# Moving DRAM sums, two gt2 steps, a pair of staging pages and one small write in a transformer block kernel

## The chip, the cores and the metric

The kernel runs on one core of one Trainium2 chip. A core has TensorE (matmuls; PE in the profile, with its weight loads as PEld), VectorE (DVE), ScalarE (ACT), GpSimd (POOL) and SyncE (SP), which here only issues DMAs. Sixteen DMA engines serve the core; DMAs are issued from the queues of SyncE, ScalarE and GpSimd, each in order. The metric is the time of one execution on the device in microseconds, from three runs and one profiled execution.

## The reference, cut to what matters

```python
mod = silu(c) @ w_ada + b_ada                      # 6 x 2048
sh1, sc1, gt1, sh2, sc2, gt2 = split(mod, 6)
h = rms_norm(x, g_mix) * (1 + sc1) + sh1
proj = h @ w_in                                    # xr, yr, q, k, v, f_logit
mix = concat(rms_norm(rglru(xr, yr)), rms_norm(forgetting_attention(q, k, v, f_logit)))
x = x + gt1 * (mix @ w_out)
h2 = rms_norm(x, g_ffn) * (1 + sc2) + sh2
gate, up = split(h2 @ w_up, 2)                     # w_up: 2048 x 11264
x = x + gt2 * ((silu(gate) * up) @ w_down)         # w_down: 5632 x 2048
```

There are 512 tokens and 2048 features, all in 32-bit floats. Each weight and each activation is split into a high and a low part (`hi` on ScalarE, `lo = raw - hi` on VectorE), and each product is three matmuls: hi by hi, hi by lo, lo by hi.

## The kernel before, in words

The work runs in one order: input projection, recurrence and attention by heads, output projection (four groups `wo0` to `wo3`), the upper product with `w_up`, the down product with `w_down`.

**The end of the output projection.** The modulation vectors come from dot products on VectorE: `ada_block` (L155) loads two pages of 512 KB of `w_ada` on SyncE's queue and multiplies them with silu(c). The last one of `SC2` gives `a2` (L902), with which `make_hr` (L905) makes the scaled input `hrh`, `hrl` of the upper product.

**The upper product.** The first 2 x 2 feature tiles are an ordinary product, two groups `up0` and `up1` (L1100), fed by `stream` (L257) through pages tagged `raw` (2 of them, 1 MB each). The other 40 feature tiles are done in 10 blocks of 4 (L1187). Each block is a 2 x 2 block product after Strassen and Winograd: seven products instead of eight, in the order 4, 5, 1, 7, 6, 2, 3. A product is eight steps j of six matmuls; two halves of four steps each. The weights of a block are four units, A, C, B and D, of two pages each (`load_unit`, L1130, SyncE's queue). `prod_weights` (L1151) loads A and C at product 4, B at product 1, D at product 2, and forms sums in place on VectorE: A += C for product 5, C += B for 7, A += B for 6, A += D for 3. Product 2 uses D itself. So C's pages come free in product 7, B's in 6, D's in 2 and A's in 3. Pages are of two kinds: `raw` (2) and `raw2` (4). `IN_RAW` says which units get `raw`: with (2, 4) modulo 8 it is B of an even block and A of an odd one.

`back` (L1175) brings the result of a block to the other layout in product 5 of the next block; `keep_act` (L1046) writes four forms of it to DRAM (`td`) on SyncE's queue.

**The DRAM sums.** The down product is also done by seven block products and needs two sums of quarters of `w_down` in DRAM (`s2d`, `s4d`), in 11 groups q. `sums24(q, n)` (L1078) issues at n = 0 four copies of 512 KB from SyncE's queue, ordered behind the last weight load that has been traced, and at n = 1, 2, 3 two adding DMAs each from GpSimd. Group 0 runs in `up0` and `up1` at `SUMS_STEPS`; the other ten in the blocks, one group every 13 halves from half 4 on (L1207).

**gt2.** The last modulation vector is made in the blocks. Its 64 pieces (4 rows r of c times 16 tiles i) are dealt out 6 or 7 to a block (`GT2_N`). Class `Gt2` (L178) loads at step (3, 3), that is product 7, step 3, up to six items from ScalarE's queue: a row of c whenever r changes, and pieces. Two items get a page with the tag `c`, the others one of four with the tag `d`, so later items must wait until a piece is used and its page comes free. `piece` runs one product on VectorE at the steps of `GT2_STEPS` ((4, 1) is product 6, step 1; 5 is product 2; 6 is product 3). Rows change in blocks 2, 5 and 7. `gt2_spread` (L1315) writes the 2048 sums to DRAM from 128 partitions (`k p -> p k`, 4-byte pieces, SyncE's queue) and reads them back spread over all partitions on GpSimd's queue.

**The down product.** `PHASES` (L1247) has four phases. In the first, products 4 and 5 alternate over 11 steps q; `dn_open` (L1262) loads per q a weight of 1 MB for each and two pages of activations from `td`. Product 4's weight goes to `raw`, product 5's to `raw2`; product 5 adds product 4's raw weight to its own (L1286), after which that `raw` page is free. One step is 24 matmuls.

**What sets the order.** The instructions of each engine and queue are put in order by a scheduler ahead of the run: by priority, among those whose inputs and pages it expects to be ready. `tc.high_priority(offset)` moves instructions up; `tc.issue_after(ins)` puts an instruction behind `ins` on its own engine and makes it wait for nothing else. On the chip each queue is in order: an instruction that waits for a page holds all behind it.

Of the kernel before, what the change touches and what calls it, by code (L numbers as in the profile page):

```python
# [54 lines left out]
STD = 2  # L55
X_STEPS = (13, 13, 13, 6)
KEEP = (2, 8, 2)
GT2_STEPS = ((4, 1), (4, 2), (4, 3), (4, 5), (4, 7), (5, 1), (5, 3))
GT2_N = (6, 6, 6, 6, 6, 6, 7, 7, 7, 7)
SUMS_AT, SUMS_PER = 4, 13  # L60
SUMS_STEPS = ((1, 8, 15), (6,))
BU_PART = (0, 5, 10, 16)
BUP_STEP = 3
NQ = FT // 4
# [7 lines left out]
def block_kernel(ctx, tc, xT, crow, adaT, vecs, bfr, w1, wyr, wqkv0, wqkv, wgate, wout, wup0, wups, wdn, outT):  # L72
# [411 lines left out]
    def add(hooks, n, *fns):  # L484
        hooks.setdefault(n, []).extend(fns)
        return hooks
# [613 lines left out]
    for gi in range(STD):  # L1100
        hk = {}
        if gi == 0:
            r1_sums, r1_spread = rstd_parts(ss1, D, "rstd_1", bank=acc)
            add(hk, BUP_STEP, up_bias_sum)
            add(hk, R1STEP[0], r1_sums)
            add(hk, R1STEP[1], lambda: r1.append(r1_spread()))
            add(hk, X_STEPS[3], lambda: x1_by_tokens(3))
        for i, n in enumerate(SUMS_STEPS[gi]):
            add(hk, n, lambda i=i + 3 * gi: sums24(0, i))
        for j in range(4):  # L1110
            add(hk, T_STEPS[gi][j], lambda j=j + 4 * gi: make_t(j))
        ps = fm_group(wup0[gi], list(range(KT)), hr, f"up{gi}", hooks=hk,
                      ps=[bank(gi + 1, f, f"up{gi}p{f}") for f in range(4)])
        up_last = lambda gi=gi, ps=ps: up_out(gi, ps)
        if gi < STD - 1:
            up_last()
# [4 lines left out]
    bp = ctx.enter_context(tc.tile_pool(name="bp", bufs=4))  # L1121

    U_A, U_C, U_B, U_D = range(4)
    IN_RAW = (2, 4)
    ORDER = (4, 5, 1, 7, 6, 2, 3)
    POST = 1900
    NBLK = (FT - 2 * STD) // 4
# [1 line left out]

    def load_unit(b, u):  # L1130
        tiles = []
        mine = len(loads) % 8 in IN_RAW
        loads.append((b, u))
        for hf in range(2):
            nm = f"uw{b}_{u}{hf}"
            if mine:
                t = wp.tile([P, 2048], F32, tag="raw", name=nm, bufs=RAW)
            else:
                t = bp.tile([P, 2048], F32, tag="raw2", name=nm)
            for i in range(2):  # L1140
                cs = slice(i * 1024, (i + 1) * 1024)
                ld = nc.sync.dma_start(out=t[:, cs], in_=wups[b, u, :, hf * 2048 + i * 1024:hf * 2048 + (i + 1) * 1024])
            up_loads.append(ld.ins)
            tiles.append(t)
        return tiles
# [39 lines left out]
    hk = {}  # L1185
    nprod = halves = 0
    for b in range(NBLK):  # L1187
# [6 lines left out]
        for i, p in enumerate(ORDER):  # L1194
# [3 lines left out]
            for j, hi, lo in prod_weights(p, b, un):  # L1198
                th, tl = T[p][j]
                for t in range(2):  # L1200
                    c_ = slice(t * P, (t + 1) * P)
                    mm(ps[t], th[:, c_], hi, j == 0, False)
                    mm(ps[t], th[:, c_], lo, False, False)
                    mm(ps[t], tl[:, c_], hi, False, j == 7)
                for fn in hk.get((i, j), ()):
                    fn()
                if j % 4 == 3:  # L1207
                    n = halves - SUMS_AT
                    halves += 1
                    if 0 <= n < SUMS_PER * (NQ - 1) and n % SUMS_PER % 3 == 0 and n % SUMS_PER < 12:  # L1210
                        sums24(1 + n // SUMS_PER, n % SUMS_PER // 3)
            if b + i == 0:
                up_last()
            if p in (4, 5, 1, 7):
# [34 lines left out]
    def dn_load(tag, blk, q, nm):  # L1249
        pool = wp if tag == "raw" else bp  # L1250
        raw = pool.tile([P, 2048], F32, tag=tag, name=nm, bufs=RAW if tag == "raw" else 4)
        src = {-2: s2d, -4: s4d}[blk][q] if blk < 0 else wdn[blk, q]
        for i in range(2):
            ld = nc.sync.dma_start(out=raw[:, i * 1024:(i + 1) * 1024], in_=src[:, i * 1024:(i + 1) * 1024])
        dn_loads.append(ld.ins)
        return raw

# [4 lines left out]
    def dn_open(ph, q):  # L1262
        prods = PHASES[ph]
        with tc.high_priority(offset=AHEAD):
            raws, ts = [], []
            for n, (p, blk, ix) in enumerate(prods):
                nm = f"dq{p}_{q}"
                raws.append(dn_load("raw2" if n or (len(prods) == 1 and q % 2) else "raw", blk, q, nm + "r"))
                tl, th = page(nm + "tl", "h"), page(nm + "th", "h")
                nc.sync.dma_start(out=tl, in_=td[ph][q][:, ix])  # L1270
                ts.append((th, tl))
        opened[ph, q] = raws, ts

# [40 lines left out]

    def gt2_spread():  # L1315
        gd = drp.tile([KT, P], F32, name="gt2d")
        nc.sync.dma_start(out=gd.rearrange("k p -> p k"), in_=mods[GT2])
        gv = gd.rearrange("(a k) p -> a k p", k=4)
        for a in range(4):
            g = page(f"gt2b{a}", "c")  # L1320
            nc.gpsimd.dma_start(out=g.rearrange("p (k m) -> p k m", k=4), in_=gv[a:a + 1].broadcast_to([P, 4, P]))
            gt2b.append(g)
# [25 lines left out]
    for ph, prods in enumerate(PHASES):  # L1348
# [8 lines left out]
        for q, n in steps:  # L1357
# [12 lines left out]
                    for f in TAIL_AT[q, k]:  # L1370
                        up_tail[f]()
            if n == 0:
                if (ph, q) == (0, 2):
                    gt2_spread()
        if ph == 0:
            q4, q5 = copies(ps[4], "q4_"), copies(ps[5], "q5_")
# [92 lines left out]
```

## Time and profile before

| | us |
|---|---|
| three runs | 2070.52, 2060.04, 2062.78 (median 2062.78) |
| profiled execution | 2061.59 |
| its span, first to last instruction | 2059.7 |
| TensorE busy | 2017.1 |
| VectorE busy | 1674.8 |
| ScalarE busy | 987.2 |
| GpSimd busy | 107.0 |

The mean granted TensorE clock was 0.992. The profile takes the span from the first instruction on; its page shows busy time by engine, the span in slices, the DMA queues, the chain of work that ended last and the costliest groups. Waits are listed as "engine, operation, line <- what ended the wait: total, times, longest". Windows show, for a stretch of time, each engine's busy time with its number of instructions, the granted clock (1.00 is full speed), the share of the DMA engines' time that was busy, and GB/s. A queue is written SPq or ACTq. `L255` is the matmul line, `L250` and `L251` are the two splits.

### The profile page before, as it was taken

What the parts mean: (1) busy time and instruction counts of PE and PEld (TensorE: products, weight loads), DVE (VectorE), ACT (ScalarE), POOL (GpSimd) and SP (SyncE); (2) the same over time, 40 slices, a digit from 0 to 9 for tenths busy, and PEclk for the clock granted to TensorE, in tenths of its full rate; (3) what the DMA queues carried; (4) which work ended last, traced back from release to release, by engine and by line L of the source; (5) the groups of instructions that cost most, each with busy time, mean ns of one, the idle gap of its engine ahead of it and who ended that gap; (6) DMA issues with size and microseconds to landing.
All of it is one profiled execution on the core that took longest, in us unless ns stands there. A gap on an engine that the chain in (4) does not pass through costs nothing.

```text
span 2059.7 us, 25583 instructions
## 1 busy us (share of the span) xinstructions
PE 2017.1 (98%) x9329; PEld 1695.0 (82%) x9329; DVE 1674.8 (81%) x2300; ACT 987.2 (48%) x1361; POOL 107.0 (5%) x138
## 2 busy tenths in 40 slices
PE   9999999999999989999999999999999899999999
PEld 7889998888888868888888877888778788888887
DVE  8999778986687659898798797887978877777796
ACT  4433447764522247544544444544445445545443
POOL 0000001111000000000000000000100100000000
PEclk9999999999999999999999999999999999999999
DMA  9989766667588884877977877596965577777793
GB/s 352 357 298 333 240 219 224 227 217 245 189 279 310 308 259 154 212 179 237 252 188 236 226 221 238 166 280 214 233 226 177 164 259 239 260 248 264 254 329 124
DMA packets 175714, 496.32 MB, mean 241 GB/s; under 512 B 20482, under 2 KB 43170, under 8 KB 171491
## 3 DMA queue, kind: packets, MB, share of 16 engines
q1 hardware_dynamic: 153316, 434.80, 61.6%
q0 software_dynamic: 11040, 39.59, 10.8%
q10 hardware_dynamic: 11232, 20.30, 2.8%
q8 instruction: 73, 1.20, 0.2%
q14 instruction: 53, 0.43, 0.1%
HBM read 458.93 MB, written 93.36 MB: 268 GB/s over the span
## 4 chain that ended last, share of the span: by engine, by line
PE 72%; DVE 9%; DMA 9%; issue 8%; ACT 1%; POOL 1%; SPq 0%; DVEq 0%; POOLq 0%; ACTq 0%
PE up_2p L255 5%; PE up_5p L255 5%; PE up_4p L255 5%; PE up_3p L255 5%; PE w1p L255 4%; PE up_1p L255 4%; PE up_7p L255 4%; DMA ada<-in_adaT 4%; PE up_6p L255 3%; PE dn6p L255 3%; PE dn3p L255 3%; PE dn1p L255 3%; PE dn2p L255 3%; PE dn7p L255 3%; PE dn5p L255 3%
## 5 line engine op out<-in xcount | busy, mean ns | idle before, releaser
L1149 DVE TENSOR_TENSOR uw<-uw,uw 128x2048 f32<-128x2048 f32 x80 | 182.6, 2282 | 0.0
L163 DVE SCALAR_TENSOR_TENSOR ada<-ada,c_b 128x1024 f32<-128x1024 f32 x96 | 116.2, 1220 | 43.3 <-DMA ada<-in_adaT 42.9
L250 ACT ACTIVATE up_0h<-uw 128x1024 fp32r<-128x1024 f32 x70 | 74.3, 1061 | 121.5 <-PE up_2p L255 23.6
L250 ACT ACTIVATE up_1h<-uw 128x1024 fp32r<-128x1024 f32 x70 | 74.4, 1063 | 108.4 <-PE up_6p L255 18.4
L251 DVE TENSOR_TENSOR up_0l<-uw,up_0h 128x1024 fp32r<-128x1024 f32 x70 | 85.4, 1220 | 35.3 <-ACT up_0h L250 35.3
L250 ACT ACTIVATE up_3h<-uw 128x1024 fp32r<-128x1024 f32 x70 | 74.4, 1063 | 79.7 <-PE up_2p L255 23.6
L251 DVE TENSOR_TENSOR up_1l<-uw,up_1h 128x1024 fp32r<-128x1024 f32 x70 | 85.3, 1219 | 30.3 <-ACT up_1h L250 30.3
L251 DVE TENSOR_TENSOR up_2l<-uw,up_2h 128x1024 fp32r<-128x1024 f32 x70 | 85.3, 1219 | 22.7 <-ACT up_2h L250 22.7
L250 ACT ACTIVATE up_2h<-uw 128x1024 fp32r<-128x1024 f32 x70 | 74.2, 1060 | 58.2 <-PE up_2p L255 16.6
L251 DVE TENSOR_TENSOR up_3l<-uw,up_3h 128x1024 fp32r<-128x1024 f32 x70 | 85.3, 1218 | 14.7 <-ACT up_3h L250 14.7
L1076 POOL DMA_DIRECT2D s2d<-in_wdn x44 | 36.6, 872 | 726.5 <-DMA s2d<-in_wdn 726.5
L201 DVE SCALAR_TENSOR_TENSOR gt<-gt,gt_None 128x512 f32<-128x512 f32 x64 | 43.1, 685 | 15.9 <-DMA gt<-in_adaT 15.9
L255 PE MATMUL w1p<-hpl,w1h 128*128 128x512 f32 x128 | 49.8, 389 | 0.0
L255 PE MATMUL w1p<-hph,w1l 128*128 128x512 f32 x128 | 49.8, 389 | 0.0
L255 PE MATMUL w1p<-hph,w1h 128*128 128x512 f32 x128 | 42.5, 392 | 0.0
L173 DVE SCALAR_TENSOR_TENSOR ada<-ada,c_b 128x1024 f32<-128x1024 f32 x32 | 39.0, 1218 | 4.1 <-ACT c_b L126 4.1
L173 DVE SCALAR_TENSOR_TENSOR adf<-adf,c_b 128x1024 f32<-128x1024 f32 x32 | 39.0, 1219 | 0.3 <-DMA adf<-in_adaT 0.2
L609 ACT ACTIVATE bt<-bt,nm 128x128 f32<-128x128 f32 (+3 forms) x32 | 18.0, 561 | 40.0 <-DVE nm L607 39.7
L688 DVE SCALAR_TENSOR_TENSOR ba<-bw,sh,ba 128x512 f32<-128x512 f32 x45 | 32.5, 746 | 3.8 <-DMA bw<-in_w 2.4
L954 DVE SCALAR_TENSOR_TENSOR bu_acc<-bu,mod,bu_acc 128x512 f32<-128x512 f32 x30 | 22.5, 748 | 13.5 <-DMA bu<-in_wup 13.0
L255 PEld LDWEIGHTS w1p<-hph,w1h 128*128 128x128 f32 x128 | 24.0, 188 | 5.4 <-ACT hph L416 0.3
L255 PEld LDWEIGHTS w1p<-hpl,w1h 128*128 128x128 f32 x128 | 24.0, 188 | 5.0
(2290 smaller groups left out, 6641.1 us busy)
## 6 DMA issues: line engine op xcount, KB each, us to landing
uw<-in_wups SPq DMA_DIRECT2D x160, 512.0 KB, 6.4
ada<-in_adaT SPq DMA_DIRECT2D x128, 512.0 KB, 5.7
s2d<-in_wdn POOLq DMA_DIRECT2D x44, 512.0 KB, 8.1
adf<-in_adaT SPq DMA_DIRECT2D x32, 512.0 KB, 6.4
gt<-in_adaT ACTq DMA_DIRECT2D x64, 256.0 KB, 6.2
s2d<-in_wdn SPq DMA_DIRECT2D x22, 512.0 KB, 10.5
s4d<-in_wdn SPq DMA_DIRECT2D x22, 512.0 KB, 9.9
s4d<-s2d POOLq DMA_DIRECT2D x22, 512.0 KB, 8.5
```

The costliest lines, as they stand in the source:

```text
L163: nc.vector.scalar_tensor_tensor(out=t, in0=t, scalar=1.0, in1=cs, op0=ALU.mult, op1=ALU.mult, accum_out=ac)
L173: nc.vector.scalar_tensor_tensor(out=t, in0=t, scalar=1.0, in1=c_b[:, cs], op0=ALU.mult, op1=ALU.mult, accum_out=ada_acc[j][:, hf, i:i + 1])
L201: nc.vector.scalar_tensor_tensor(out=t, in0=t, scalar=1.0, in1=c, op0=ALU.mult, op1=ALU.mult, accum_out=gt2_acc[:, r, i:i + 1])
L250: tail_hi.append(nc.scalar.activation(R(hi[:, :n]), raw_ap, AF.Copy).ins)
L251: tail_lo.append(nc.vector.tensor_sub(R(lo[:, :n]), raw_ap, hi[:, :n]).ins)
L255: nc.tensor.matmul(ps, lhsT=R(l), rhs=R(r), start=start, stop=stop)
L609: nc.scalar.activation(p[:, :n], p[:, :n], AF.Exp, scale=-1.0, bias=nm, accum_out=sm)
L688: nc.vector.scalar_tensor_tensor(out=ba[j], in0=src, scalar=s1, in1=ba[j], op0=ALU.mult, op1=ALU.add)
L954: nc.vector.scalar_tensor_tensor(out=a, in0=src, scalar=s2, in1=a, op0=ALU.mult, op1=ALU.add)
L1076: nc.gpsimd.dma_start(out=out[:, cs], in_=src[:, cs], accum_op=ALU.add)
L1149: nc.vector.tensor_add(d_, d_, s_)
```

## The change

It has four parts.

1. The DRAM sums of group 0 leave `up0` and `up1`; all 11 groups run in the blocks, one every 12 halves from half 2 on.
2. The sixth gt2 piece of a block moves from step (5, 1) to (5, 5), the seventh from (5, 3) to (6, 1).
3. Units C and D of every block get the `raw` pages, A and B the `raw2` pages; each weight load is ordered behind the load traced before it (A, C and B of block 0 only behind the first streamed load), and all loads of the down product behind the last one of the upper product.
4. `gt2_spread` is called at step (0, 4) of the down product, not (0, 2), and its write is ordered behind the last down weight load traced by then.

```diff
-GT2_STEPS = ((4, 1), (4, 2), (4, 3), (4, 5), (4, 7), (5, 1), (5, 3))
+GT2_STEPS = ((4, 1), (4, 2), (4, 3), (4, 5), (4, 7), (5, 5), (6, 1))
 GT2_N = (6, 6, 6, 6, 6, 6, 7, 7, 7, 7)
-SUMS_AT, SUMS_PER = 4, 13
-SUMS_STEPS = ((1, 8, 15), (6,))
+SUMS_AT, SUMS_PER = 2, 12
...
-        for i, n in enumerate(SUMS_STEPS[gi]):
-            add(hk, n, lambda i=i + 3 * gi: sums24(0, i))
...
-    IN_RAW = (2, 4)
+    IN_RAW = (1, 3)
...
-        mine = len(loads) % 8 in IN_RAW
+        mine = len(loads) % 4 in IN_RAW
...
-                ld = nc.sync.dma_start(out=t[:, cs], in_=wups[b, u, :, ...])
+                with tc.issue_after(up_loads[-1] if b or u == U_D else stream_loads[0]):
+                    ld = nc.sync.dma_start(out=t[:, cs], in_=wups[b, u, :, ...])
...
-                    if 0 <= n < SUMS_PER * (NQ - 1) and n % SUMS_PER % 3 == 0 and n % SUMS_PER < 12:
-                        sums24(1 + n // SUMS_PER, n % SUMS_PER // 3)
+                    if 0 <= n < SUMS_PER * NQ and n % SUMS_PER % 3 == 0 and n % SUMS_PER < 12:
+                        sums24(n // SUMS_PER, n % SUMS_PER // 3)
...
# dn_load, and the td load in dn_open
+            with tc.issue_after(up_loads[-1]):
...
# gt2_spread
-        nc.sync.dma_start(out=gd.rearrange("k p -> p k"), in_=mods[GT2])
+        with tc.issue_after(dn_loads[-1]):
+            nc.sync.dma_start(out=gd.rearrange("k p -> p k"), in_=mods[GT2])
...
-                if (ph, q) == (0, 2):
+                if (ph, q) == (0, 4):
                     gt2_spread()
```

More of the change, by code (lines that the diff above doesn't have):

```diff
@@ L1141, in load_unit @@
                 cs = slice(i * 1024, (i + 1) * 1024)
-                ld = nc.sync.dma_start(out=t[:, cs], in_=wups[b, u, :, hf * 2048 + i * 1024:hf * 2048 + (i + 1) * 1024])
+                with tc.issue_after(up_loads[-1] if b or u == U_D else stream_loads[0]):
+                    ld = nc.sync.dma_start(out=t[:, cs], in_=wups[b, u, :, hf * 2048 + i * 1024:hf * 2048 + (i + 1) * 1024])
             up_loads.append(ld.ins)
@@ L1253, in dn_load @@
         for i in range(2):
-            ld = nc.sync.dma_start(out=raw[:, i * 1024:(i + 1) * 1024], in_=src[:, i * 1024:(i + 1) * 1024])
+            with tc.issue_after(up_loads[-1]):
+                ld = nc.sync.dma_start(out=raw[:, i * 1024:(i + 1) * 1024], in_=src[:, i * 1024:(i + 1) * 1024])
         dn_loads.append(ld.ins)
@@ L1269, in dn_open @@
                 tl, th = page(nm + "tl", "h"), page(nm + "th", "h")
-                nc.sync.dma_start(out=tl, in_=td[ph][q][:, ix])
+                with tc.issue_after(up_loads[-1]):
+                    nc.sync.dma_start(out=tl, in_=td[ph][q][:, ix])
                 ts.append((th, tl))
```

## Prediction

> **What bounds the kernel now.** I read the page first, then TensorE's waits, then a table of windows cut at the start of each upper block product, then the chain of waits and SyncE's queue at the places where a window is too long.
>
> ```profile
> span 2059.7 us, 25583 instructions
> PE 2017.1 (98%) x9329; PEld 1695.0 (82%) x9329; DVE 1674.8 (81%) x2300; ACT 987.2 (48%) x1361; POOL 107.0 (5%) x138
> ```
>
> TensorE is the bound: 98% busy, 42.6 us of idle in the whole span. No part of the change adds or removes a matmul. So the change can only take away or bring waits of TensorE, and the slow matmuls that follow a wait.
>
> ```profile
> PE up0p L255 <- ACT hrh L908: 8.0, 1, 8.0
> PE dn4p L255 <- ACT dq_0w0h L250: 4.0, 1, 4.0
> 730.00:736.00 6.00, 2.16 (x4) 1.45 (x5) 5.64 (x11) 2.94 (x5) 1.22 (x2) 0.51 1.02 181
> 733.84 14.41 PE up0p L255 x48
> 1673.82 5.44 PE dn4p L255 x24
> 983.24:1061.39 78.15, 78.15 (x353) 64.58 (x353) 67.47 (x76) 38.30 (x44) 4.95 (x6) 1.00 0.80 226
> 1139.50:1219.38 79.88, 78.96 (x354) 64.40 (x353) 67.42 (x75) 38.07 (x44) 9.07 (x11) 1.00 0.94 251
> 1219.38:1303.41 84.03, 79.81 (x353) 65.53 (x353) 67.82 (x76) 38.20 (x44) 4.95 (x6) 0.98 0.74 218
> 1303.41:1381.61 78.20, 78.20 (x353) 64.50 (x353) 68.07 (x77) 38.41 (x44) 4.92 (x6) 1.00 0.74 217
> 1381.61:1466.89 85.28, 81.23 (x353) 65.97 (x353) 68.38 (x78) 38.20 (x44) 4.94 (x6) 0.96 0.74 220
> 1466.89:1546.69 79.80, 78.73 (x354) 64.43 (x353) 68.06 (x77) 38.10 (x44) 4.92 (x6) 1.00 0.81 226
> 1546.69:1627.00 80.31, 78.88 (x352) 64.00 (x351) 65.99 (x76) 36.56 (x43) 0.00 (x0) 1.00 0.47 139
> 1627.00:1755.40 128.40, 124.13 (x545) 101.73 (x546) 98.23 (x92) 65.78 (x82) 7.46 (x12) 0.99 0.75 256
> ```
>
> In a window's row stand its length, the engines' busy times, the granted clock, the DMA share and GB/s. A dense block takes 78.15 us (block 2). Blocks 4, 5, 7 and 8 take 1.73, 5.88, 7.13 and 1.65 us more: 16.4 us. Blocks 6 (78.20) and 2 lose nothing. Dense matmuls come 5.44 us per 24. In the standard product before the blocks, TensorE waits 8.0 us, and its next 48 matmuls take 14.41 us in place of 10.88, at a granted clock of 0.51: 11.5 us lost. The last two rows hold block 9 and the first phase of the down projection: 208.71 us, where a block (78.15), 22 steps of 5.44 and 16 transposes (1.74 by the row of 8 quoted below) make 199.6; 9.1 us lost. These three places, 37 us, are what the change can touch.
>
> **Part 1: the first group of DRAM sums leaves the standard product.**
>
> ```profile
> 705.02 0.63 SPq L1083 DMA_DIRECT2D s2d<-in_wdn  x1
> 711.05 1.47 SPq L152 DMA_DIRECT2D ada<-in_adaT  x2
> 685.22 8.73 DMA ada<-in_adaT
> 703.51 5.38 DMA ada<-in_adaT
> 712.19 17.88 DMA ada<-in_adaT
> 733.07 0.73 ACT hrh L908
> ada<-in_adaT SPq DMA_DIRECT2D x128, 512.0 KB, 5.7
> 712.00:718.00 6.00, 6.00 (x28) 4.96 (x27) 1.39 (x3) 1.06 (x1) 1.76 (x2) 1.00 1.03 347
> 722.64 1.12 ACT L924 ACTIVATE x1w<-x1p 128x512 f32<-128x512 f32 x2
> ```
>
> The chain of waits into the 8.0 us runs: last ada load (17.88 us, where the one before took 5.38 and the median is 5.7), two VectorE products, the modulation sum, hrh on ScalarE, TensorE. The four copies of 512 KB went out from 705.02 on, ahead of that load, and the DMA engines are full (share 1.03). The load itself cannot go earlier than 711.05, since its page is freed by VectorE then. With the copies gone it lands after 5.4 to 8.7 us (8.73 is the dearest of the ada loads ahead of it in the chain), at 718 to 721. hrh followed the landing by 3.0 us (712.19 + 17.88 to 733.07), so it could start at 721 to 724. ScalarE is busy with x1w until 723.76. TensorE's last matmul before the gap ends at 733.84 - 8.0 = 725.8. So the wait goes, and with it the slow clock: 11.5 us saved. If 1 us of wait remained, 10.5; never under 8.0 unless another wait ends late. What is late next is hrh behind x1w on ScalarE, about 2 us ahead of TensorE's need, less 0.7 for hrh itself.
>
> [...]
>
> **Part 2: eleven groups in the blocks, and later gt2 steps.** A group's four copies go on SyncE's queue right behind the weight load that was last when the group came up, and GpSimd adds as data land. By halves of a product (4+13n before, 2+12n after), they stand behind C in blocks 1 to 4, D in 4 to 7, B in 0 and 8 now; behind C in 0, 1, 6, 7, D in 1, 2, 7, 8 and B in 3, 4, 5 after.
>
> ```profile
> 1265.49 10.55 DMA gt<-in_adaT
> 1276.13 0.69 DVE L201 SCALAR_TENSOR_TENSOR gt<-gt,gt_None 128x512 f32<-128x512 f32 x1 [4.97 <-DMA gt<-in_adaT]
> 1429.37 12.96 DMA gt<-in_adaT
> 1442.43 0.69 DVE L201 SCALAR_TENSOR_TENSOR gt<-gt,gt_None 128x512 f32<-128x512 f32 x1 [4.05 <-DMA gt<-in_adaT]
> ```
>
> A group behind D puts its copies just ahead of the gt2 loads that reuse pages: they take 10.55 and 12.96 us, VectorE stands 4.97 and 4.05 us, and the splits behind it starve TensorE. Which piece it is differs. Blocks 2, 5 and 7 cross from one row of c to the next and load one row more. In block 5 the fifth piece waits, at step (4,7), which the change leaves; in block 7 the sixth, at (5,1), which goes to (5,5): four steps of six matmuls, or 5.44 us, later. That covers the 4.05. In the same way the sixth and seventh pieces of the other blocks are covered. On VectorE the pieces only trade places with the sums after product 6; the matmuls hide it, or else it costs up to 0.7 us per piece.
>
> After the change a D group meets a crossing in block 2 (fifth piece reused, as in block 5 now) and block 7. I price by the rows: block 2 as block 5 (5.88), block 7 and block 1 as block 4, which also has a C and a D group (1.73 each), blocks 3 and 5 (a B group behind a busy block) as block 8 (1.65 each), 4, 6 and 8 nothing. That makes 12.6 in place of 16.4: 3.8 saved. From both sides: if block 2 is also free and the rest cheap, 14 saved; if each D group costs 7.13, more lost than now (the third rival).
>
> **Part 3: pages of C and D, chained loads.** The pages of a unit are freed by the same splits as before, so each load waits for the same instruction. C of block 0 now takes the standard stream's pages, as B did; the last of it goes out where B's did (815.18, and earlier by what part 1 saves). Block 0 starts at 827 or later (983.24 less two blocks of at most 78.15), and C is wanted by its second product, 48 matmuls or 10.9 us on: nothing, hidden by product 4; without that cover it would be some 6 us once (5.7 for 512 KB). The loads' forced order (A, C, B, D) is the order in which pages come free: nothing. What it changes is the end: the pages for product 4's first two down weights are then D's, not A's.
>
> ```profile
> 815.18 0.81 SPq L1142 DMA_DIRECT2D uw<-in_wups  x2
> 1607.07 0.80 SPq L1254 DMA_DIRECT2D dq_2r<-in_wdn  x2
> 1614.19 0.38 SPq L1317 DMA_DIRECT2D gt2d<-mod  x1
> 1615.96 0.80 SPq L1254 DMA_DIRECT2D dq_0r<-in_wdn  x2
> 1622.00:1624.00 2.00, 2.00 (x10) 1.66 (x9) 0.41 (x1) 0.00 (x0) 0.00 (x0) 1.00 0.41 12
> gt2d<-mod SPq DMA_DIRECT2D x1, 8.0 KB, 12.3
> 1629.11 1.06 ACT dq_0w0h L250
> 1638.24 0.87 PE up_t L1178 x8
> 1645.70 0.81 SPq L1254 DMA_DIRECT2D dq_4r<-in_wdn  x2
> 1653.40 0.82 SPq L1254 DMA_DIRECT2D dq_3r<-in_wdn  x2
> 1687.16 0.81 SPq L1254 DMA_DIRECT2D dq_6r<-in_wdn  x2
> 1695.42 0.61 PE L255 MATMUL dn4p<-dq_6w0h,dq_6th 128*128 128x512 f32 x2
> ```
>
> Today product 4's first weight goes out at 1615.96, when A's page is freed, 1.8 us behind the gt2 write (8 KB in 4-byte pieces), which takes 12.3 us to land while the engines move 12 GB/s. ScalarE gets the weight at 1629.11, and TensorE waits the 4.0 us of the row above. D's page is freed at 1607.07 (product 5's third weight goes into it today). So after the change product 4's first weight goes out then, with no write ahead of it, and is there long before 1627: the start of the phase costs nothing.
>
> **Part 4: the gt2 write behind more loads.** It is now ordered behind the last load traced at step (0,4): product 5's fifth weight (1645.70 here). The next on SyncE is product 4's fourth weight, 7.7 us later (1653.40), for it waits for a page. The write would go out 0.8 us behind the former, so it blocks the queue for 12.3 - 6.9 = 5.4 us of that load's time, and the load lands 2.6 us after the block's end (as at 1615.96: 1614.19 + 12.3 = 1626.5, ScalarE begins 1629.11): 8.0 us after its issue. In the dense phase TensorE uses such a weight 8.26 us after the issue (1687.16 to 1695.42), and the splits take some 2.3 of that, an estimate from ScalarE's 1.06 with VectorE's step a little longer. So TensorE waits 2.0 us; or 5.0, if the weight of 1 MB issued just ahead holds the write up first (3.0 us at the 347 GB/s of the row in part 1). At the other end the block is hidden altogether. I take 3.5, and 2 us for block 9's VectorE and the clock: 5.5 of 9.1 lost remain, 3.6 saved (from -2 to 9).
>
> [...]
>
> **Sum.** 11.5 + 3.8 + 3.6 = 18.9 us off the profiled execution's 2061.6, or 2042.7; the median of the three runs (2062.8) is 1.2 above that execution: 2044.
>
> **The rivals.** 0.5% (10.3 us) is about what a measurement of this kernel can tell from no change.
>
> *The standard product keeps its wait.* hrh also needs ScalarE and VectorE, and the next two weights of 1 MB use the same queue; if the wait only shortens by 3 us, the sum is 18.9 - 8.5, or 2052.4. Against it: the load alone is out of line (17.88 against 5.7).
>
> *Almost all waits go.* The D groups drift past the gt2 loads and the write is hidden: 11.5 + 14 + 6 = 31.5 us, 2031. For it: block 6 has a D group and loses 0.05.
>
> *The D groups cost what the dearest does.* Four of them (blocks 1, 2, 7, 8) at 7.13 and the B groups of 3, 4 and 5 at 1.65 are 33.5 us where 16.4 are lost now: 17.1 more, against 15.1 gained elsewhere, 2065: slower. It turns slower where a D group costs over 6.6 us, and measurably at 9.2. Against it: blocks 4 and 6 have one and lose 1.73 and 0.05.
>
> *The write does not get behind what matters.* Ahead of it stand weights that are wanted late, behind it the one that is wanted next; if the block of 12.3 us comes through whole, the phase's start loses 12.3 where 9.1 was lost, 3.2 more: 2051.
>
> **How the numbers follow.** Forecast 0.60, wait kept 0.14, almost all gone 0.10, dear D groups 0.08, write in the way 0.08. The forecast's own range is 2036 to 2052 (parts 2 and 4 by their bounds, not both at once). 2033 to 2056 takes in half of the second rival and most of the first and last. Faster by over 0.5% (under 2052.5): 0.58 + 0.10 + 0.05 + 0.04 = 0.77. Same: 0.19. Slower by over 0.5%: half of the third rival, 0.04.
>
> **What would show it.** Right: no wait of up0p for hrh, its first 48 matmuls in 10.9 us, the last ada load in under 9 us; block 5 at 80 us or less and block 7 at 80; block 2 at 84; dn4p without a wait for dq_0; the gt2 write between product 5's fifth and product 4's fourth weight, and one wait of dn4p for dq_3 behind it. Wrong: up0p still waiting over 3 us; D groups costly in blocks 1 and 8; a new wait of over 6 us in the first phase.

## The result, and the profile after

The kernel after takes 2044.2 us, the median of four runs (2042.37 to 2046.33); the kernel before took 2061.9 beside it (2060.04 to 2070.52). The ratio is 0.9906, with a 95% interval of 0.9877 to 0.9936. The profiled execution of the kernel after took 2044.69 us. In its line numbers everything behind the changed constants stands one lower (the matmul line is L254).

The page, first its span and TensorE:

```profile
span 2043.0 us, 25569 instructions
PE 2012.8 (99%) x9329; PEld 1693.9 (83%) x9329; DVE 1676.8 (82%) x2300; ACT 987.4 (48%) x1361; POOL 104.7 (5%) x138
```

The span is 16.7 us shorter; TensorE is idle for 30.2 us of it in place of 42.6, and its busy time is 4.3 us shorter at an equal number of matmuls, with a mean granted clock of 0.995 in place of 0.992.

**The standard product.** SyncE's queue, its last load of `ada`:

```profile
714.04 1.47 SPq L151 DMA_DIRECT2D ada<-in_adaT  x2
```

The chain of waits (start, us, what):

```profile
728.82 10.88 PE up0p L254 x48
```

The load goes out 14.8 us ahead of `up0`; no wait stands there any more, and its first 48 matmuls take 10.88 us where they took 14.41.

**The blocks and the first down phase.** Windows cut at the first matmul of each block (1 to 5, 7 and 9 are shown), then the first and the second down phase. The columns are those of the prediction's windows, length first:

```profile
896.36:974.48 78.12, 78.12 (x353) 64.57 (x352) 67.67 (x75) 38.24 (x44) 8.23 (x10) 1.00 0.88 249
974.48:1053.34 78.86, 78.39 (x353) 64.49 (x352) 67.59 (x76) 38.41 (x44) 4.94 (x6) 1.00 0.75 219
1053.34:1139.02 85.68, 81.49 (x353) 65.33 (x352) 67.62 (x75) 37.92 (x44) 5.73 (x7) 0.98 0.85 231
1139.02:1217.13 78.11, 78.11 (x354) 64.57 (x352) 67.59 (x75) 38.41 (x44) 4.94 (x6) 1.00 0.82 221
1217.13:1296.15 79.02, 78.39 (x354) 64.50 (x352) 67.51 (x76) 38.39 (x44) 5.76 (x7) 1.00 0.85 239
1374.31:1452.71 78.40, 78.40 (x354) 64.44 (x352) 68.01 (x78) 38.40 (x44) 8.22 (x10) 1.00 0.91 252
1530.87:1609.00 78.13, 78.13 (x354) 64.57 (x352) 68.83 (x79) 39.25 (x46) 1.24 (x2) 1.00 0.63 204
1609.00:1738.48 129.48, 124.51 (x546) 102.26 (x544) 95.70 (x90) 63.10 (x79) 7.48 (x12) 0.97 0.75 232
1738.48:1858.18 119.70, 119.70 (x530) 99.07 (x528) 90.47 (x78) 59.27 (x72) 0.00 (x0) 1.00 0.73 248
```

A block without a wait takes 78.13 us. Blocks 5, 7 and 8, which lost 14.7 us before, now lose 1.2; block 2 loses 0.7; block 3, which lost nothing, loses 7.6. Blocks 0 to 8 lose 9.5 us in place of 16.6 (these windows begin a tenth of a microsecond elsewhere than the prediction's, which is why 16.4 became 16.6). Block 9 and the first down phase take 207.6 us, 8.0 over the 199.6 that the prediction worked out; before they lost 9.1.

**Where the down phase waits now.** TensorE's longest wait, then the chain into it:

```profile
PE dn4p L254 <- ACT dq_3w0h L249: 4.9, 1, 4.9
```

```profile
1629.76 12.13 DMA dq_3r<-in_wdn
```

gt2's write on SyncE's queue and the read on GpSimd's of what was written, in order of time:

```profile
1621.98 0.54 SPq L1318 DMA_DIRECT2D gt2d<-mod  x1
1639.86 2.21 POOL L1322 DMA_DIRECT2D gt2b<-gt2d  x4 [13.38 <-DMA gt2d<-mod]
```

Two windows, while the write is under way and after the wait:

```profile
1628.00:1632.00 4.00, 4.00 (x19) 3.30 (x19) 2.79 (x2) 2.02 (x2) 0.00 (x0) 1.00 1.30 54
1642.00:1648.00 6.00, 4.86 (x11) 3.36 (x12) 4.84 (x4) 2.63 (x3) 0.07 (x1) 0.50 1.03 413
```

`dn4p` no longer waits for its first weight (`dq_0`) but for its fourth (`dq_3`), issued 7.8 us behind gt2's write. The write goes out at 1621.98, and its reader is released at 1639.86, 17.9 us later. In the first window the DMA engines are busy (share 1.30) and move 54 GB/s. After the wait the clock is at 0.50 for some 6 us.

**Block 3.** SyncE's queue around the end of block 2 (the first copies of two groups), then GpSimd's last sums of the earlier group, of the later one and, for comparison, of the group after that:

```profile
1020.95 0.57 SPq L1082 DMA_DIRECT2D s2d<-in_wdn  x1
1049.75 0.50 SPq L1082 DMA_DIRECT2D s2d<-in_wdn  x1
1054.78 0.82 POOL L1075 DMA_DIRECT2D s4d<-s2d  x1 [3.00 <-DMA s2d<-in_wdn]
1088.43 0.81 POOL L1075 DMA_DIRECT2D s4d<-s2d  x1 [5.06 <-DMA s2d<-in_wdn]
1161.56 0.81 POOL L1075 DMA_DIRECT2D s4d<-s2d  x1 [2.43 <-DMA s2d<-in_wdn]
```

The two longest pieces of the chain into the wait:

```profile
1081.71 12.23 DMA td<-tu
1093.97 11.14 DMA gt<-in_adaT
```

A group behind D (from 1020.95) and a group behind the next block's B (from 1049.75) stand 29 us apart; the other neighbours begin 59 to 86 us apart. The earlier group's last sum goes out at 1054.78, when the later group's copies are already in flight. The later group's last sum goes out at 1088.43, 38.7 us behind its first copy; the next group, also behind a B but alone, needs 26.2 (1135.40 to 1161.56). So the later group's sums still run when block 3 writes `td`. A write of `td` then takes 12.23 us, the gt2 load that gets its page another 11.14, and the splits behind them on ScalarE and VectorE come late (ScalarE stands 3.13 and 4.73 us ahead of two of them).

**What differs without the change.** TensorE reached `up0` at 725.8 before and at 728.8 after, 3.0 us later, though up to there the DMA queues differ only by the six transfers of group 0 (705 to 717), which the change takes away. Among the traces of this study it came there between 724.7 and 731.4. Most of this lies in the attention stage, behind which TensorE came at 494.5 in place of 491.5; the window from 200 to 500 us, first in the kernel after:

```profile
200.00:500.00 300.00, 288.51 (x1563) 265.39 (x1562) 240.61 (x456) 177.81 (x327) 28.85 (x34) 0.98 0.69 230
```

And in the third experiment below, which came to `up0` at 724.7:

```profile
200.00:500.00 300.00, 290.47 (x1578) 266.61 (x1577) 242.17 (x459) 178.71 (x327) 31.54 (x35) 0.99 0.71 231
```

TensorE does 2.0 us more work there in the second. In the span, then, the 16.7 us are 11.5 (standard product) + 7.1 (blocks 0 to 8) + 1.1 (block 9 and first down phase) - 3.0 (run to run).

### The profile page after: what moved, and what is told of

It is laid out like the page before. It is cut to its first block, busy times and chain, and to the rows that moved or that the text cites. A ratio compares the mean times of both kernels' runs of the same rounds, so it can differ in the third digit from the quotient of the medians.

```text
span 2043.0 us, 25569 instructions
## 1 busy us (share of the span) xinstructions
PE 2012.8 (99%) x9329; PEld 1693.9 (83%) x9329; DVE 1676.8 (82%) x2300; ACT 987.4 (48%) x1361; POOL 104.7 (5%) x138
## 4 chain that ended last, share of the span: by engine, by line
PE 81%; issue 7%; DVE 6%; DMA 4%; POOL 1%; ACT 1%; SPq 0%; DVEq 0%; POOLq 0%; ACTq 0%
PE up_2p L254 5%; PE up_3p L254 5%; PE up_5p L254 5%; PE up_4p L254 5%; PE up_1p L254 5%; PE w1p L254 4%; PE up_7p L254 4%; PE up_6p L254 4%; PE dn6p L254 3%; PE dn3p L254 3%; PE dn1p L254 3%; PE dn2p L254 3%; PE dn7p L254 3%; PE dn4p L254 3%; PE dn5p L254 3%
## 5 line engine op out<-in xcount | busy, mean ns | idle before, releaser
L249 ACT ACTIVATE up_0h<-uw 128x1024 fp32r<-128x1024 f32 x70 | 74.3, 1062 | 115.6 <-PE up_7p L254 18.9
L250 DVE TENSOR_TENSOR up_0l<-uw,up_0h 128x1024 fp32r<-128x1024 f32 x70 | 85.5, 1222 | 30.2 <-ACT up_0h L249 29.9
L250 DVE TENSOR_TENSOR up_3l<-uw,up_3h 128x1024 fp32r<-128x1024 f32 x70 | 85.4, 1220 | 12.3 <-ACT up_3h L249 12.3
L254 PE MATMUL w1p<-hph,w1l 128*128 128x512 f32 x128 | 49.8, 389 | 0.0
L254 PE MATMUL w1p<-hpl,w1h 128*128 128x512 f32 x128 | 49.8, 389 | 0.0
L254 PE MATMUL w1p<-hph,w1h 128*128 128x512 f32 x128 | 42.5, 392 | 0.0
L953 DVE SCALAR_TENSOR_TENSOR bu_acc<-bu,mod,bu_acc 128x512 f32<-128x512 f32 x30 | 22.5, 749 | 12.9 <-DMA bu<-in_wup 12.5
L415 ACT ACTIVATE hph<-x,A 128x512 fp32r<-128x512 f32 x16 | 11.6, 723 | 36.0 <-DVE A L412 36.0
L620 ACT ACTIVATE pT<-pt 128x512 f32<-128x512 f32 (+3 forms) x32 | 13.2, 435 | 31.8 <-PE pt L616 31.8
```

The costliest lines, as they stand in the source:

```text
L249: tail_hi.append(nc.scalar.activation(R(hi[:, :n]), raw_ap, AF.Copy).ins)
L250: tail_lo.append(nc.vector.tensor_sub(R(lo[:, :n]), raw_ap, hi[:, :n]).ins)
L254: nc.tensor.matmul(ps, lhsT=R(l), rhs=R(r), start=start, stop=stop)
L620: nc.scalar.activation(pT[:, qs], pt[:, qs], AF.Copy)
L953: nc.vector.scalar_tensor_tensor(out=a, in0=src, scalar=s2, in1=a, op0=ALU.mult, op1=ALU.add)
```

## The experiments

Ten kernels were run. What each loses, from windows like those above, is in this table; "b9 + phase 1" is what block 9 and the first down phase take over 199.6 us, "std" the wait ahead of `up0` and the slow clock behind it. A dense block counts 78.13 us (block 0: 76.16), which leaves some 0.2 us open in a sum over nine blocks. Medians are of 4 to 10 runs, of one run where marked.

| kernel | median | std | blocks 0-8 | of it block 3, 4 | b9 + phase 1 | phase 2 |
|---|---|---|---|---|---|---|
| before | 2061.9 | 11.5 | 16.6 | 0.0, 1.7 | 9.1 | 0 |
| after | 2044.2 | 0 | 9.5 | 7.6, 0.0 | 8.0 | 0 |
| 1: before + sums | 2050.7 | 0 | 13.6 | 4.4, 0.0 | 8.4 | 0 |
| 2: after, write in rows | 2031.0 | 0 | 5.7 | 4.9, 0.0 | 0.0 | 0.3 |
| 3: after, old gt2 steps | 2041.6 | 0 | 9.6 | 7.4, 0.0 | 7.7 | 0 |
| 4: after, old pages | 2047.1 | 0 | 10.0 | 6.3, 0.0 | 9.9 | 0 |
| 5: before + write moved | 2060.5 (one) | 10.5 | 15.9 | 0.1, 0.0 | 9.1 | 0 |
| 6: after, write from ScalarE | 2040.2 (one) | 0 | 8.4 | 7.1, 0.0 | 7.6 | 0 |
| 7: after, a group every 13 halves | 2042.3 | 0 | 7.8 | 0.0, 6.5 | 6.8 | 0 |
| 8: rows, groups spread | 2028.4 | 0 | 1.4 | 0.0, 0.0 | 0.2 | 0.2 |
| 9: after, late write in pieces | 2040.7 | 0 | 8.6 | 7.3, 0.2 | 0.0 | 4.5 |
| 10: before + sums + pages | 2050.5 | 0 | 15.9 | 6.4, 2.2 | 7.8 | 0 |

**1. The sums alone.** The kernel before with part 1 and the new places of the groups; pages, order, gt2 steps and write as before.

```diff
-SUMS_AT, SUMS_PER = 4, 13
+SUMS_AT, SUMS_PER = 2, 12
-        for i, n in enumerate(SUMS_STEPS[gi]):
-            add(hk, n, lambda i=i + 3 * gi: sums24(0, i))
```

> The kernel before with part 1 of the change alone (all eleven groups of sums in the blocks, every 12 halves from half 2). Theory: TensorE's wait before the first standard product goes, and with it the slow clock behind it: 11.5 us saved there. The gt2 write still stands ahead of the first down weight: dn4p waits about 4 us for dq_0 and the first down phase takes 128 us. With the old pages the copies of a D group stand between the two halves of the next block's unit A, ahead of the gt2 loads: blocks 1 and 7 lose 2 to 7 us each, all blocks together 12 to 19, as before. Time 2050 (2046 to 2053). Rival: the sums' new place is all there is to the change, blocks and down phase included: 2044.

2050.66 us (2046.3 to 2054.5, ten runs), ratio 0.9954 (0.9939 to 0.9969). The chain of waits at the start of `up0`:

```profile
725.88 10.88 PE up0p L254 x48
```

The standard product loses nothing, which is the whole of part 1's 11.5 us, shown with this part alone. The blocks still lose 13.6 of 16.6 us, 5.1 of them in block 7, but only 0.7 in block 1, for which 2 to 7 had been expected. The profiled execution (2046.34) was among the fastest of the ten, so its blocks are rather on the cheap side.

**2. gt2's write in rows.** The kernel after, with the 128 x 16 sums transposed on TensorE and written as 16 rows of 512 bytes in place of 2048 pieces of 4. The scheduler put it later as well, into the second down phase.

```diff
+        pt = rgp("gt2t")
+        nc.tensor.transpose(out=pt[:KT, :P], in_=mods[GT2], identity=ident)
+        gt2row = cp.tile([P, P], F32, name="gt2row")
+        nc.vector.tensor_copy(out=gt2row[:KT, :], in_=pt[:KT, :P])
-            nc.sync.dma_start(out=gd.rearrange("k p -> p k"), in_=mods[GT2])
+            nc.sync.dma_start(out=gd, in_=gt2row[:KT, :])
```

> The changed kernel with the gt2 write made of 16 rows of 512 bytes (TensorE transposes the 128x16 sums first, VectorE copies them out) in place of 2048 pieces of 4 bytes, at the same place in the queue. Theory: the 4-byte pieces are what held up product 4's fourth weight; the wait of dn4p for dq_3 (4.9 us, and the slow clock behind it) goes, the first down phase takes 122 to 123.5 us in place of 129.5, and the time falls by 6 to 7: 2038. Rival: the fourth weight is late because its page comes free late; the wait stays, 2044.

2030.99 us (2030.45 to 2032.36), ratio 0.9855 (0.9831 to 0.9879): 13 us less than the kernel after, where 6 to 7 had been expected. The windows of block 3, of the first and of the second down phase:

```profile
1051.32:1134.33 83.01, 80.95 (x354) 65.50 (x352) 67.62 (x75) 38.17 (x44) 5.73 (x7) 0.98 0.87 235
1603.50:1724.99 121.49, 121.49 (x545) 100.76 (x544) 95.61 (x90) 62.99 (x79) 5.29 (x8) 1.00 0.71 240
1724.99:1844.95 119.96, 119.96 (x530) 98.95 (x529) 90.74 (x79) 59.39 (x72) 2.19 (x4) 1.00 0.75 255
```

The first down phase is dense: 121.49 us, all of it busy, 8.0 less. The rest of the 13 us lies where the write cannot reach: 3.8 in blocks 0 to 8 and 1.7 ahead of `up0` in these profiles. Up to there the DMA queues of the two kernels have the same order, so this is a difference between executions; but the four runs of each kernel lie closer together than that, and where it comes from is not shown. Form and place of the write were both changed; experiments 6 and 9 take them apart.

**3. The old gt2 steps.**

```diff
-GT2_STEPS = ((4, 1), (4, 2), (4, 3), (4, 5), (4, 7), (5, 5), (6, 1))
+GT2_STEPS = ((4, 1), (4, 2), (4, 3), (4, 5), (4, 7), (5, 1), (5, 3))
```

> The changed kernel with the old gt2 steps (sixth piece at (5,1), seventh at (5,3)). Theory: the later steps only matter where a reused page is refilled late, which now is block 7 alone (D group and a change of rows): 2 to 4 us more there, the other blocks as in the changed kernel; 2046.5. Rival A: the later steps are what freed the blocks: blocks 5 and 7 or those with a D group (1, 2, 7, 8) lose 4 to 7 each again, 2052 or more. Rival B: they do nothing: 2044.

2041.59 us (2040.72 to 2043.75), ratio 0.9907 (0.9882 to 0.9931). My theory fell: the blocks lose 9.6 us, as with the new steps (9.5), and block 7, whose sixth piece the later step was to cover, loses nothing:

```profile
1370.80:1448.93 78.13, 78.13 (x354) 64.57 (x352) 68.22 (x78) 38.23 (x44) 8.22 (x10) 1.00 0.92 256
```

VectorE waits 0.9 us for gt2 loads in this block, where it waited 5.2 in the kernel before, and TensorE does not feel it; so part 2's later steps cover nothing.

**4. The old pages.** The kernel after with B and A alternately in the `raw` pages, as before; the forced order of the loads is kept.

```diff
-    IN_RAW = (1, 3)
+    IN_RAW = (2, 4)
-        mine = len(loads) % 4 in IN_RAW
+        mine = len(loads) % 8 in IN_RAW
```

> The changed kernel with the old choice of pages (B of an even and A of an odd block in the raw pages), its chained load order kept. Theory: in blocks 1 and 7 the copies stand again between the halves of the next block's unit A, ahead of the gt2 loads, and the blocks lose 2 to 4 us more each; product 4's first weight goes out about 9 us later than in the changed kernel, when A's page comes free, but with no write ahead of it and lands in time (dn4p waits under 1 us for dq_0); 2048. Rival A: the pages bring nothing by themselves: 2044. Rival B: the late page alone costs the start of the down product 3 us or more, whatever the write does.

2047.12 us (2041.40 to 2049.86), ratio 0.9931 (0.9908 to 0.9954). Blocks 0 and 9:

```profile
822.94:900.43 77.49, 76.79 (x337) 62.91 (x336) 69.48 (x77) 36.53 (x41) 0.81 (x1) 1.00 0.50 161
1534.15:1614.61 80.46, 78.92 (x353) 64.34 (x352) 68.64 (x79) 39.19 (x46) 1.48 (x2) 1.00 0.61 193
```

Block 9 is 2.3 us longer than in the kernel after, and block 0, 76.16 without a wait, 1.3. The pages are worth 2 to 3 us (2.4 by the table, 2.9 by the medians, whose runs overlap), mostly at the two ends of the row of blocks. The theory's 2 to 4 us each in blocks 1 and 7 did not come: both lose nothing. That TensorE does not wait for `dq_0` was as expected.

**5. The write moved, alone.** The kernel before with part 4.

```diff
-        nc.sync.dma_start(out=gd.rearrange("k p -> p k"), in_=mods[GT2])
+        with tc.issue_after(dn_loads[-1]):
+            nc.sync.dma_start(out=gd.rearrange("k p -> p k"), in_=mods[GT2])
-                if (ph, q) == (0, 2):
+                if (ph, q) == (0, 4):
```

> The kernel before with part 4 alone: gt2's write of 2048 pieces goes behind product 5's fifth weight load instead of behind product 4's fourth. In the kernel before, the last block and the first down phase lost 5.6 and 3.6 us to it, 9.1 us together. The prediction's theory (behind more loads the write meets less): 5.5 us together, about 3.6 us less. Theory after the experiments on form, place and queue (the pieces delay whatever load is next behind them by about the same time): the loss of the block moves into the phase, block 9 loses 0 to 2.5 us, the phase 7 to 9 us, together 8 to 11 us, no gain over 1.5 us. The std product's wait of about 8 us and the losses of the other blocks stay as before.

One run of 2060.5 us beside 2061.0 for the kernel before. TensorE's two longest waits:

```profile
PE up0p L255 <- ACT hrh L908: 8.4, 1, 8.4
PE dn4p L255 <- ACT dq_3w0h L250: 4.8, 1, 4.8
```

Block 9 and the first down phase:

```profile
1545.33:1625.35 80.02, 78.92 (x354) 64.35 (x352) 68.72 (x79) 39.22 (x46) 0.00 (x0) 1.00 0.49 169
1625.35:1754.00 128.65, 123.86 (x545) 101.78 (x544) 95.63 (x90) 63.09 (x79) 7.48 (x12) 0.97 0.76 237
```

Block 9 loses 1.9 us in place of 5.6, the phase 7.2 in place of 3.6: 9.1 together, exactly what the kernel before loses. Part 4 by itself moves a loss and removes none.

**6. The write from ScalarE's queue.**

```diff
-        with tc.issue_after(dn_loads[-1]):
-            nc.sync.dma_start(out=gd.rearrange("k p -> p k"), in_=mods[GT2])
+        with tc.issue_after(tail_hi[-1]):
+            nc.scalar.dma_start(out=gd.rearrange("k p -> p k"), in_=mods[GT2])
```

> The kernel after, with gt2's write of 2048 pieces of 4 bytes issued from ScalarE's queue instead of SyncE's, at about the same time of the first down phase. In the kernel after, product 4's fourth weight came late behind this write and the first down phase lost 8.0 us. Theory of the queue (the loads wait because they stand behind the write on SyncE's own queue): the fourth weight lands in its usual time and the first down phase loses 0 to 2 us, so the span is 6 to 8 us shorter than that of the kernel after, about 2036. Theory of the engines (the small pieces hold the 16 DMA engines, whichever queue they come from): the loss stays at 6 to 10 us, span about 2043. A third way: ScalarE's own splits, queued behind the issue, come late, which would also show as a loss, but with ScalarE and no DMA named in the waits.

One run of 2040.23 us. The write on ScalarE's queue and the read on GpSimd's:

```profile
1642.68 0.39 ACTq L1318 DMA_DIRECT2D gt2d<-mod  x1
1657.13 2.21 POOL L1322 DMA_DIRECT2D gt2b<-gt2d  x4 [35.01 <-DMA gt2d<-mod]
```

Three weight loads in the chain:

```profile
1625.89 5.57 DMA dq_3r<-in_wdn
1637.40 5.12 DMA dq_4r<-in_wdn
1647.77 11.59 DMA dq_5r<-in_wdn
```

The first down phase:

```profile
1604.74:1733.85 129.11, 124.17 (x546) 102.00 (x544) 95.60 (x90) 62.98 (x79) 7.50 (x12) 0.97 0.72 234
```

The write went out 37.9 us into the phase, where it was 13.0 in the kernel after. Product 4's fourth and fifth weights, ahead of it, take 5.57 and 5.12 us; the sixth, issued on SyncE's queue 5.1 us behind it, takes 11.59, and the phase loses 7.6 us. So a load need not stand behind the write on the same queue to come late: the write is on ScalarE's, the load of 11.59 us on SyncE's. ScalarE stood 9.08 us waiting for that load, so its own splits were not what came late, the expectation's third way.

**7. A group every 13 halves.** With it the 29 us between two groups move from blocks 2 and 3 to blocks 3 and 4.

```diff
-SUMS_AT, SUMS_PER = 2, 12
+SUMS_AT, SUMS_PER = 0, 13
```

> The kernel after, with a group of DRAM sums every 13 half products from the first, instead of every 12 from the third. By the queue order, the groups then follow the loads of C in block 0, D in blocks 0 to 3 and B in blocks 4 to 9, and the one place where two groups stand less than 30 us apart is between blocks 3 and 4 (in the kernel after: between blocks 2 and 3, where block 3 lost 8 us). Theory (two groups close to each other on the queue are what costs): block 3 loses at most 1 us, block 4 loses 5 to 9 us, the other blocks under 1 us each, time 2044 (2040 to 2048). Rival (block 3 loses for a reason of its own, such as the pages of its loads): block 3 still loses 5 us or more and block 4 nothing. Second rival (a group behind B is dear by itself): blocks 4 to 9 lose over 1 us each, time 2050 or more.

2042.29 us (2039.14 to 2044.47), ratio 0.9901 (0.9875 to 0.9926). Blocks 3, 4 and 5:

```profile
1050.89:1129.05 78.16, 78.16 (x353) 64.57 (x352) 67.71 (x75) 38.21 (x44) 4.92 (x6) 1.00 0.73 225
1129.05:1213.64 84.59, 81.92 (x354) 66.50 (x352) 67.80 (x75) 37.77 (x44) 5.76 (x7) 0.96 0.84 231
1213.64:1291.85 78.21, 78.21 (x353) 64.49 (x352) 67.61 (x76) 38.41 (x44) 4.93 (x6) 1.00 0.81 225
```

The longest piece of the chain in block 4:

```profile
1158.69 16.67 DMA td<-tu
```

The loss has moved with the neighbours: block 3 is free, block 4 loses 6.5 us, with the same `td` write (16.67 us) in its chain. Five more blocks with a group behind B lose at most 0.4 each, so such a group is not dear by itself.

**8. Rows, and the groups spread.** The write of experiment 2; group 0 in the second standard product, the others at halves of their own. On SyncE's queue no group then begins less than 53.7 us behind the one before it (29 in the kernel after).

```diff
-SUMS_AT, SUMS_PER = 2, 12
+SUMS_STEPS = (0, 4, 8, 12)
+SUMS_AT = (2, 10, 24, 38, 52, 66, 80, 94, 108, 122)
...
+        for i, n in enumerate(SUMS_STEPS if gi else ()):
+            add(hk, n, lambda i=i: sums24(0, i))
...
+                    for q, at in enumerate(SUMS_AT, 1):
+                        if halves - at in (0, 3, 6, 9):
+                            sums24(q, (halves - at) // 3)
```

> The kernel with gt2's write in rows of 512 bytes, and the groups of DRAM sums at places of their own: the first in the second std product, then behind the loads of C and D of block 0 and of D of blocks 1 to 8, so that no two stand less than 45 us apart. Theory (only neighbours cost): no block loses over 1.5 us, all ten together at most 3 us, the std products lose nothing, the first down phase loses nothing: 2026 (2023 to 2030). Rival (each group costs by its own transfers, wherever it stands): the blocks lose 5 us or more together, 2031 or more. Second rival (the first group again delays the loads of the std product, as in the kernel before): a wait of over 1 us in the std products, 2030 or more.

2028.42 us (2026.78 to 2032.43), ratio 0.9840 (0.9809 to 0.9870). All ten blocks lose 1.4 us together, 1.0 of it in block 0, and the two standard products nothing. It is the fastest kernel of the study: 33 us below the kernel before, about 16 below the kernel after, and 2.6 below experiment 2, from which it differs by the places of the groups alone (one of its four runs, 2032.43, lies above all of experiment 2's). The only wait of TensorE that the view lists from 700 to 2020 us:

```profile
PE up_4p L255 <- DVE up_3l L251: 0.3, 1, 0.3
```

Block 3:

```profile
1052.29:1130.44 78.15, 78.15 (x353) 64.57 (x352) 67.62 (x75) 38.39 (x44) 4.95 (x6) 1.00 0.75 223
```

**9. The write in pieces, but late.** The kernel after with its write of 4-byte pieces in the second down phase, near where the rows of experiment 2 went out.

```diff
-                if (ph, q) == (0, 4):
+                if (ph, q) == (1, 2):
```

> The kernel after, with gt2's write still in 2048 pieces of 4 bytes on SyncE's queue, but issued in the second down phase, one load ahead of where the write in rows stood. The write in rows saved 13 us and changed two things, form and place. Theory of the form (the small pieces delay whatever load is queued behind them): the second down phase loses 4 to 8 us in place of the first, time 2040 to 2044. Theory of the place (loads of the second phase are issued long enough ahead that a delay of 12 to 18 us does not reach TensorE): no loss in either phase, time 2033 to 2037.

2040.70 us (2037.99 to 2043.78), ratio 0.9894 (0.9869 to 0.9920). The first and the second down phase:

```profile
1607.84:1729.33 121.49, 121.49 (x546) 100.76 (x544) 95.59 (x90) 62.99 (x79) 5.32 (x8) 1.00 0.70 239
1729.33:1853.52 124.19, 121.87 (x530) 100.06 (x529) 90.48 (x78) 59.25 (x73) 2.19 (x4) 0.99 0.73 247
```

The longest wait in the second:

```profile
PE dn1p L254 <- ACT dq_2w0h L249: 1.8, 1, 1.8
```

The first phase is dense and the second loses 4.5 us. The write stands one weight load earlier on the queue than the rows of experiment 2, ahead of `dq_2` and not behind it. From issue to landing the two writes took, rows first:

```profile
gt2d<-gt2row SPq DMA_DIRECT2D x1, 8.0 KB, 4.5
gt2d<-mod SPq DMA_DIRECT2D x1, 8.0 KB, 14.0
```

The next down weights behind the rows landed in 4.1 to 6.2 us, those behind the pieces in 9.3 to 12.4. So at nearly the same place the pieces cost 4.5 us and the rows 0.3: the form is what costs. The place decides between 8 and 4.5.

**10. Sums and pages without the forced order.** Experiment 1 with the new pages. On SyncE's queue the next block's A now stands ahead of D in every block: four weight loads go out some 25 us into a block and four more from 34 us on, and in block 9, which no A follows, D's go out at 34.

```diff
-    IN_RAW = (2, 4)
+    IN_RAW = (1, 3)
-        mine = len(loads) % 8 in IN_RAW
+        mine = len(loads) % 4 in IN_RAW
```

> The kernel before with the new places of the DRAM sums and the new pages (C and D of a block in the same pages), but without the forced order of the loads. The queue then has the next block's A ahead of D in nearly every block, because A's pages (B's of this block) are planned to come free first, and gt2's write behind product 5's second weight. The prediction held the forced order to be worth nothing: by that, this is the kernel after with gt2's write elsewhere, 2044 to 2050. Theory now (the order is what the pages need: with A first, D's load waits on the queue until product 6 has read B, about 11 us before D is needed, and comes late in many blocks): the ten blocks lose 20 us or more together, most of it as a wait of product 2 for D's splits, and the time is 2055 or more.

2050.52 us (2046.60 to 2054.80), ratio 0.9943 (0.9921 to 0.9964). The time lies between the two forecasts: the blocks lose 15.9 us and not 20 or more, but 6.4 us more than with the order. Blocks 4 and 7, which lose 0.0 and 0.3 in the kernel after:

```profile
1140.99:1221.28 80.29, 79.23 (x353) 64.29 (x352) 67.38 (x75) 38.04 (x44) 4.94 (x6) 1.00 0.79 214
1380.11:1460.89 80.78, 78.42 (x354) 64.53 (x352) 68.22 (x78) 38.40 (x44) 9.04 (x11) 1.00 0.96 254
```

Against experiment 1 the pages alone bring nothing (2050.5 and 2050.7); with the order but the old pages (experiment 4) it is 2047.1, with both, the kernel after, 2044.2.

## Why the prediction was right in the sum, point by point

**Part 1** (11.5 us): right in size and cause. Experiment 1 has it alone, with nothing lost in the standard product, and experiment 5, without it, keeps a wait of 8.4 us. The slow stretch behind the wait is 3.5 us of it, by the rows of 14.41 and 10.88 us, and that is what came back. In experiment 5 the same 48 matmuls behind the wait of 8.4 us take 13.01 us, so there the slow stretch costs 2.1.

**Part 2** (3.8 us saved) failed in its step "block 2 as block 5 (5.88)" and in "blocks 3 and 5 ... 1.65 each". Block 2 lost 0.7 and block 3 lost 7.6. I had priced each group by the load that it stands behind, and by whether it meets a change of the row of c; experiment 7 shows that what counts in this kernel is the distance to the neighbouring group, and experiment 8 that with at least 53.7 us between any two all blocks together lose 1.4 us, D groups in nine blocks included. I had the positions of all groups and did not subtract them from each other. The distance is not what blocks 5 and 7 lost by in the kernel before: its groups begin 42 us apart or more, and the one in block 5 came 74 us behind its neighbour. What freed these two blocks was not part 2 alone, since experiment 1 still loses 5.1 us in block 7. That the later gt2 steps cost nothing was right; that they cover 4.05 us in block 7 was wrong (experiment 3).

**Part 3**: "the forced order is the order in which pages come free: nothing" was the other failed step, and with it "each load waits for the same instruction". B's pages come free before C's, and not after them, as the order of the products has it: in experiment 10, which has the new pages without the order, the first four loads of a block go out at 25 us and not at 34. In the kernel before, by the kinds of its pages, D of an odd block took a page of B, and of an even block a page of C, behind the next block's A; the last D went out 25 us into block 9 (1571.76), in the kernel after 34 us into it (1565.31). No row that I quoted told this. What the order is worth shows where it is the main difference left, since experiments 3 and 5 gain nothing by the gt2 steps and the place of the write: 2047.1 in place of 2050.7 with the old pages (experiments 4 and 1, whose runs overlap), 2044.2 in place of 2050.5 with the new (the kernel after and experiment 10, whose runs do not). Block 7 loses 0.0 and 0.3 us with the order, 5.1 and 2.6 without it. How much of the rest is the order's stays open, since block 3 alone scatters from 4.9 to 7.6 in kernels with equal groups. That the start of the down phase becomes free (no wait for `dq_0`) was right: block 9 loses nothing, and with the old pages 2.3 us.

**Part 4** (3.6 us saved): the place was right, product 4's fourth weight behind the write, and one wait of `dn4p` for it. The size was not: "I take 3.5, and 2 us" stands against 8.0. The write took 17.9 us to release its reader where I had 12.3, and the load behind it 12.13 where I had some 8; behind the wait of 4.9 us the granted clock was 0.50 (1642 to 1648). I had carried the write's duration over from its old place: there it releases its reader after 12.5 to 12.9 us in all three kernels that have it there (before, experiments 1 and 10), at the new place after 17.7 to 18.1 in all five (after, experiments 3, 4, 5 and 7). Why it takes longer there is not shown. By itself part 4 saves nothing (experiment 5), half way between the forecast's 3.6 saved and the last rival's 3.2 lost; and with the new pages but the write at its old place, block 9 and the first phase lose 7.8 (experiment 10) where the kernel after loses 8.0, so the 1.1 us gained there are not part 4's either. From ScalarE's queue the write took 14.5 us to release its reader (experiment 6, 1642.68 to 1657.13).

**The sum.** Forecast were 11.5 + 3.8 + 3.6 = 18.9 us off the profiled execution; its span fell by 11.5 + 7.1 + 1.1 - 3.0 = 16.7, and the medians came out within 0.2 us of the forecast. That is luck beside one sound term: the blocks gave 3.3 us more than forecast, the write 2.5 less, and the two errors nearly cancel; the attention stage's scatter of some 3 us from run to run is as large as either.

**The rivals.** The standard product did not keep its wait. Neither did D groups cost what the dearest does: when alone they cost at most the 1.4 us that all ten blocks of experiment 8 lose. What "almost all waits go" promised (2031) was there to be had, but by other means: rows in place of pieces and distance between groups.

## What to carry to other kernels

In this kernel block 3 lost 7.6 us to a group of copies 29 us behind another (the kernel after), and all ten blocks together 1.4 where no group began less than 53.7 us behind the one before it (experiment 8). So list the places of the transfers that run beside the main work and look for the two that are closest, before pricing each by its neighbours on the queue. Moving the small write alone left the loss of block 9 and the first down phase at 9.1 us (experiment 5); at nearly one place it cost 4.5 us in 4-byte pieces and 0.3 in rows of 512 bytes (experiments 9 and 2). So look at the bytes per piece of such a write first, and change the form. The write released its reader after 12.5 to 12.9 us at one place of the queue and after 17.7 to 18.1 at another, so don't carry a duration from one place to another. When a prediction is the sum of several terms, test the terms one by one even if the sum comes out right.

## What the hardware showed that I had not expected

Behind 8 KB written in 4-byte pieces, a weight load issued on another engine's queue took 11.59 us where the one ahead of the write took 5.12 (experiment 6); in the kernel after, the DMA engines move 54 GB/s at a busy share of 1.30 for 4 us of such a write (1628 to 1632). Behind a wait of 4.9 us the granted clock was 0.50 over the next 6 us (the kernel after, 1642 to 1648). And equal work on equal queues, everything ahead of `up0` in these kernels, came out up to 6.7 us apart from one execution to the next (`up0` at 724.7 to 731.4), more than most terms of this change.
